# The down projection's seven block products: sums into the residual by accumulating transfers instead of by VectorE

## The chip, the cores and the metric

The kernel runs on one core of one Trainium2 chip. The metric is the device time of one execution in microseconds (us), as the median of several executions. In the profile the engines are called PE (TensorE's matmuls), PEld (TensorE's weight loads), DVE (VectorE), ACT (ScalarE), POOL (GpSimd) and SP (SyncE, which issues most transfers).

## The reference

A decoder trunk of two layers on 512 tokens of width 1024. Each layer has a mixer (a gated spatial mixer in layer 0, sliding-window attention in layer 1), a gated MLP with a causal depthwise convolution of width 3, and a gated per-layer embedding, each added to the residual `h`. The change touches the MLP's down projection alone:

```python
def conv_ffn(xn, w_up, conv_w, conv_b, w_down):
    h = xn @ w_up                                   # 1024 -> 2 x 2816
    hp = jnp.pad(h, ((0, 0), (CONV_WIDTH - 1, 0), (0, 0)))
    c = conv_b + sum(hp[:, t:t + S] * conv_w[t] for t in range(CONV_WIDTH))
    g, u = jnp.split(c, 2, axis=-1)
    return (jax.nn.silu(g) * u) @ w_down            # 2816 -> 1024
...
    h = h + conv_ffn(rmsnorm(h, norm_ffn[i]), ...)
```

## The kernel before

Everything is kept transposed: features on the 128 partitions, the 512 tokens along the row. The residual is eight tiles `h[0]` to `h[7]` of 128x512 float32 in SBUF. To reach float32 accuracy each operand is split into a high and a low part (`wh`, `wl` for weights: L197 the high part by a cast on ScalarE, L198 the rest by a subtraction on VectorE), and each product is three matmuls (L229).

Weights come as a planned list of pieces of up to 1 MB, loaded by SP's queue into three staging buffers (`wraw`, L167) and split into units of up to 1024 columns, four of which can be held at once (`WBUFS`). `pump` splits four units ahead of the one in use, so a split that is late by less than that lead stops nobody.

The 22 feature blocks of the MLP are handled in three parts of 8, 8 and 6 (`PARTS`). In a part, `up` makes two PSUM tiles per block, `gated` (L547 on) applies norm, convolution and gate, and then the part is projected down and added to the residual. The last part uses plain products (`dense_add`). The first two parts of each layer use `woven_add`: a matrix product of 2x2 blocks by seven block products instead of eight. There are four such stages in the program (two layers, two parts). A stage runs over four quarters `c`; a quarter makes two of the residual's tiles, `top` = `h[2c]` and `low` = `h[2c+1]`. Its weight sums (`wsum`, L157 to L159) are made by VectorE, too.

Each of the seven products is 12 matmuls of 128x128 on 256 columns. Two PSUM tiles take them: `chain` (in the profile `dx`, 256 columns) collects products 1, 6, 7 and 4 on top of each other, and ScalarE copies what stands in it between them: `head` after product 1 (first half, L509) and after 6 (second half, L514), `tail` after 7 (second half, L523) and after 4 (first half, L496). `other` (`dy`, 512 columns) holds product 2 in its first half and product 5 in its second, and product 3 goes on top of product 5. So product 3 cannot start before somebody has read the second half (L513 before), product 7 not before the second copy into `head`, and product 4 not before the first copy into `tail`. VectorE subtracts the second half of `other` from `low` (L513), adds `head` and `other` to `top` (L524, L525) and subtracts `tail` from `low` (L497). The fourth product of a quarter is put off into the next quarter (`late`), and the gate of the next part's first block stands after quarter 0 (`between`).

The tiles `head` (tag `acc`) and `tail` (tag `sq`) have two buffers each, so a quarter reuses those of two quarters before; the gate's tiles `c` use the tags `c0` and `c1`, two buffers each. The scheduler decides the order of each engine's instructions when the program is built; on the chip each engine goes through its list in that order and waits on semaphores.

Of the kernel before, what the change touches and what calls it, by code (L numbers as in the profile page):

```python
# [8 lines left out]
F32 = mybir.dt.float32  # L9
F32R = mybir.dt.float32r  # L10
AF = mybir.ActivationFunctionType
ALU = mybir.AluOpType

P = 128
D = 1024
S = 512
# [8 lines left out]
N = S // 2  # L25
# [25 lines left out]
def tile_yoco(ctx: ExitStack, tc: tile.TileContext, t, out: bass.AP, out_b: bass.AP):  # L51
    nc = tc.nc
# [7 lines left out]
    tp = ctx.enter_context(tc.tile_pool(name="tp", bufs=2))  # L60
# [4 lines left out]
    def psum(name):  # L65
        return mmp.tile([P, S], F32, tag="mm", name=name)
# [106 lines left out]
    def pump(upto):  # L173
        while state["unit"] < min(upto, len(units)):
            i, q, lo, n = units[state["unit"]]
            load(i + 1)
            u = state["unit"]
            own = pieces[i][3]
            if own:
                pool, *tags = own[q]  # L180
                wh, wl = (pool.tile([P, n], F32R, tag=tg, name=f"own{u}_{tg}") for tg in tags)
            else:
                wh = wp.tile([P, UNIT], F32R, tag="wh", bufs=WBUFS, name=f"wh{u}")
                wl = wp.tile([P, UNIT], F32R, tag="wl", bufs=WBUFS, name=f"wl{u}")
            if i in woven:
                src = weave(i, q)
                hi, low = (x[:, :n].rearrange("p (b k m) -> p b k m", b=src.shape[1], m=P) for x in (wh, wl))
            elif i in paired:
                whole = raws[i][:, : pieces[i][1]].rearrange("p (c k n) -> p k c n", c=2, n=256)
                src = whole[:, lo // S : (lo + n) // S]  # L190
                hi, low = (x[:, :n].rearrange("p (k c n) -> p k c n", c=2, n=256) for x in (wh, wl))
            else:
                src, hi, low = raws[i][:, lo : lo + n], wh[:, :n], wl[:, :n]
            if u == 0:
                cast = nc.vector.tensor_copy(hi, src)
            else:
                cast = nc.scalar.copy(hi, src)  # L197
            state["split"] = splits[u] = cast, nc.vector.tensor_sub(low, src, hi.bitcast(F32))  # L198
            ready[u] = (wh, wl, n)
            state["unit"] += 1  # L200

    def take():
        u = state["next"]
        pump(u + 1)
        state["next"] += 1
        return ready.pop(u)
# [11 lines left out]
    def mm3(ps, parts, xs, c0, n=P, first=True, last=True, lows_last=False, onto=False):  # L218


        todo = []
        for (wh, wl, off), (xh, xl) in zip(parts, xs):
            hi, low = (w[:, off + c0 : off + c0 + n] for w in (wh, wl))
            todo.append([(hi, xh), (hi, xl), (low, xh)])
        if lows_last:
            todo = [[t[j] for t in todo for j in (0, 2)], [t[1] for t in todo]]
        todo = [x for t in todo for x in t]
        for j, (w, x) in enumerate(todo):
            nc.tensor.matmul(ps, w, x, start=first and j == 0, stop=last and j == len(todo) - 1,  # L229
                             skip_group_check=onto)  # L230
# [19 lines left out]
    h = [hp.tile([P, S], F32, tag=f"h{k}", name=f"h{k}") for k in range(KD)]  # L250
# [25 lines left out]
    ps = psum("idle").rearrange("p (a b) -> p a b", a=4)  # L276
# [165 lines left out]
    first, second = slice(0, N), slice(N, S)  # L442
# [35 lines left out]
    def woven_add(pairs, between):  # L478


        ops = {x: [p.operand(x) for p in pairs] for x in range(1, 8)}
        n = len(pairs) * P

        def unit():
            pump(state["next"] + WBUFS)
            return take()

        def product(x, ps, w, at0, first=True):
            wh, wl = w[:2]
            mm3(ps, [(wh, wl, at0 + k * P) for k in range(len(pairs))], ops[x], 0, first=first,  # L490
                onto=not first)

        def close(c, chain, w, tail):
            def run():
                product(4, chain, w, 0, first=False)
                nc.scalar.copy(tail[:, first], chain)  # L496
                nc.vector.tensor_sub(h[2 * c + 1], h[2 * c + 1], tail)  # L497
            return run

        late = None  # L500
        for c in range(4):
            top, low = h[2 * c], h[2 * c + 1]
            chain, other = psum(f"dx{c}")[:, first], psum(f"dy{c}")
            head = tp.tile([P, S], F32, tag="acc", name=f"head{c}")
            tail = tp.tile([P, S], F32, tag="sq", name=f"tail{c}")
            w = unit()
            product(1, chain, w, 0)
            product(2, other[:, first], w, n)
            nc.scalar.copy(head[:, first], chain)  # L509
            w = unit()  # L510
            product(5, other[:, second], w, n)
            product(6, chain, w, 0, first=False)
            nc.vector.tensor_sub(low[:, second], low[:, second], other[:, second])  # L513
            nc.scalar.copy(head[:, second], chain)  # L514
            w = unit()
            if late:
                late()
            for x in (7, 3) if c == 3 else (3, 7):
                if x == 3:
                    product(3, other[:, second], w, n, first=False)  # L520
                else:
                    product(7, chain, w, 0, first=False)
                    nc.scalar.copy(tail[:, second], chain)  # L523
            nc.vector.tensor_add(top, top, head)  # L524
            nc.vector.tensor_add(top, top, other)  # L525
            late = close(c, chain, unit(), tail)
            if c == 0:
                between()
        late()

    def ffn(l, norm, nxt):
# [41 lines left out]
        for i, (j0, j1) in enumerate(PARTS):  # L573
            if i < WOVEN:
                edge = at.tile([P, PAIRS, 2, N], F32R, tag="vtl", name=f"edge{i}")
                pairs = []
                for p in range((j1 - j0) // 2):
                    pair = Pair(p, edge, f"act{i}_{p}")
                    pair.begin(up(j0 + 2 * p) if p else ahead)
                    pair.end(up(j0 + 2 * p + 1))  # L580
                    pairs.append(pair)
                pss, res = up(j1, later=True), []
                u = state["next"]
                woven_add(pairs, lambda: res.append(gated(j1, pss, (u + WBUFS + 1, u + WBUFS + 2))))
                ahead, = res
                continue
            act = [whole(SLOTS - 1, j0, ahead)]
            act += [whole(j - j0 - 1, j, up(j)) for j in range(j0 + 1, j1)]
            pe = ple_in_rows() if l else ple_in(l)
            dense_add(act, j1 - j0, nxt)  # L590
# [72 lines left out]
    for q, k0, k1 in FIRST:  # L663
# [12 lines left out]
        if (q, k1) == (0, KD):  # L676
# [7 lines left out]
            cast, low = state["split"]  # L684
# [62 lines left out]
    for c in range(4):  # L747
# [4 lines left out]
        for j in range(2):  # L752
            m = 2 * c + j
            ps = ups[j]
# [23 lines left out]
    ps = psum("turned")  # L778
    for i, (name, l) in enumerate((("ple_b_gate", 1), ("norm_final", 0))):
        c0 = VEC[name] + l * KD  # L780
# [286 lines left out]
    side = at.tile([P, 4 * S], F32, tag="vtl", name="side")  # L1067
# [290 lines left out]
```

## Time and profile before

| | |
|---|---|
| median of 3 runs | 1123.33 us (1122.11 to 1124.11) |
| the profiled execution | 1120.52 us, of which the span from first to last instruction is 1118.8 us |
| granted TensorE clock in it | 0.998 |
| PE busy | 1108.8 us, 99% of the span |
| DVE busy | 868.3 us, 78% |
| ACT busy | 568.9 us, 51% |
| POOL busy | 103.9 us, 9% |
| the four stages of seven products | from 241.9, 370.0, 798.4 and 926.8 us, some 41 us each |

How to read it: the rows of a timeline give start and duration in us, engine, line, operation, and the tiles as out<-in; a bracket tells how long the engine stood idle before the instruction and what ended that. A group row gives busy time, the mean in ns of one instruction, and the idle time before the group's instructions. Matmuls overlap: what one costs is seen from the distance between two starts, not from its duration. Therefore "busy 99%" does not say how much of the time TensorE was waiting a little between starts.

### The profile page before, as it was taken

How to read it: one execution, taken by the hardware profiler on the slowest of the kernel's cores; microseconds unless marked ns; L12 is line 12 of the kernel's file. 1: busy time of each engine (PE TensorE's matmuls, PEld its weight loads, DVE VectorE, ACT ScalarE, POOL GpSimd, SP SyncE). 2: the span in 40 equal slices, each digit the busy share in tenths (PEclk: the TensorE clock that was granted, in tenths of full speed). 3: DMA queues.
4: the chain of work that ended last, by engine and by line, in shares of the span. 5: the costliest groups of instructions: out<-in, count | busy, mean ns of one | idle time of the engine just before them, and what ended most of it. 6: DMA issues, size and time to landing. Idle time of an engine off the chain costs nothing.

```text
span 1118.8 us, 14875 instructions
## 1 busy us (share of the span) xinstructions
PE 1108.8 (99%) x5691; PEld 947.1 (85%) x5691; DVE 868.3 (78%) x1374; ACT 568.9 (51%) x936; POOL 103.9 (9%) x167
## 2 busy tenths in 40 slices
PE   9999999999999999999999999999999999999997
PEld 7888888889888998888888887888898889988876
DVE  5566449999788877657988997499997898785696
ACT  5733325545444544554656776255454445445543
POOL 1100210000000000022204451100000000000210
PEclk9999999999999999999999999999999999999999
DMA  8632313223331252333134224321244212522433
GB/s 296 135 114 76 113 48 113 76 76 123 142 113 39 76 189 69 101 113 113 63 88 132 76 57 151 111 93 71 76 151 136 90 38 76 189 85 88 148 103 86
DMA packets 35624, 118.40 MB, mean 106 GB/s; under 512 B 11800, under 2 KB 17440, under 8 KB 25056
## 3 DMA queue, kind: packets, MB, share of 16 engines
q1 hardware_dynamic: 34800, 116.19, 31.8%
q0 software_dynamic: 336, 0.79, 0.4%
q8 instruction: 45, 0.74, 0.3%
q10 hardware_dynamic: 416, 0.46, 0.1%
q14 instruction: 27, 0.22, 0.1%
HBM read 109.02 MB, written 2.11 MB: 99 GB/s over the span
## 4 chain that ended last, share of the span: by engine, by line
PE 68%; DVE 20%; ACT 4%; DMA 4%; issue 3%; POOL 0%; POOLq 0%; SPq 0%; ACTq 0%; DVEq 0%
PE up L229 26%; PE d L229 7%; PE dx L229 5%; DVE wl L198 5%; PE dy L229 4%; PE gate L229 4%; PE u L229 4%; PE q L229 3%; DVE c L558 3%; DVE c L559 2%; PE o L229 2%; DVE hs L551 2%; ACT wh L197 1%; PE v L241 1%; PE v L239 1%
## 5 line engine op out<-in xcount | busy, mean ns | idle before, releaser
L198 DVE TENSOR_TENSOR wl<-wraw,wh 128x1024 fp32r<-128x1024 f32 (+2 forms) x198 | 232.8, 1177 | 83.4 <-ACT wh L197 82.1
L197 ACT CAST wh<-wraw 128x1024 fp32r<-128x1024 f32 (+2 forms) x197 | 194.1, 990 | 147.9 <-PE up L229 56.1
L229 PE MATMUL up<-nf00h,wh 128*128 128x512 f32 x352 | 137.1, 390 | 0.0
L229 PE MATMUL up<-nf10h,wh 128*128 128x512 f32 x352 | 137.0, 389 | 0.0
L229 PE MATMUL up<-nf10l,wh 128*128 128x512 f32 x352 | 137.0, 389 | 0.0
L229 PE MATMUL up<-nf00l,wh 128*128 128x512 f32 x352 | 137.0, 389 | 0.0
L229 PE MATMUL up<-nf00h,wl 128*128 128x512 f32 x352 | 136.9, 389 | 0.0
L229 PE MATMUL up<-nf10h,wl 128*128 128x512 f32 x352 | 136.9, 389 | 0.0
L557 ACT ACTIVATE c<-hs,vec 128x512 f32<-128x512 f32 x88 | 71.6, 815 | 64.4 <-DVE hs L551 62.6
L558 DVE SCALAR_TENSOR_TENSOR c<-hs,vec,c 128x511 f32<-128x511 f32 x88 | 65.5, 747 | 20.4 <-ACT c L557 20.4
L229 PEld LDWEIGHTS up<-nf10h,wh 128*128 128x128 f32 x352 | 66.1, 188 | 13.7
L229 PEld LDWEIGHTS up<-nf00h,wl 128*128 128x128 f32 x352 | 66.1, 188 | 13.7
L229 PEld LDWEIGHTS up<-nf10l,wh 128*128 128x128 f32 x352 | 66.1, 188 | 13.7
L229 PEld LDWEIGHTS up<-nf00l,wh 128*128 128x128 f32 x352 | 66.1, 188 | 13.6
L229 PEld LDWEIGHTS up<-nf00h,wh 128*128 128x128 f32 x352 | 66.1, 188 | 13.6
L229 PEld LDWEIGHTS up<-nf10h,wl 128*128 128x128 f32 x352 | 66.1, 188 | 13.5
L559 DVE SCALAR_TENSOR_TENSOR c<-hs,vec,c 128x510 f32<-128x510 f32 x88 | 65.6, 748 | 2.2
L197 ACT CAST wh<-wsum 128x1024 fp32r<-128x1024 f32 x32 | 33.7, 1052 | 35.3 <-PE dy L229 11.3
L551 DVE TENSOR_TENSOR hs<-up,nf1rstd 128x512 f32<-128x512 f32 x44 | 30.1, 686 | 21.1 <-DMA nf1rstd<-nf1line 10.5
L551 DVE TENSOR_TENSOR hs<-up,nf0rstd 128x512 f32<-128x512 f32 x44 | 30.1, 686 | 20.9 <-DMA nf0rstd<-nf0line 10.4
L198 DVE TENSOR_TENSOR wl<-wsum,wh 128x1024 fp32r<-128x1024 f32 x32 | 39.1, 1221 | 9.3 <-ACT wh L197 9.2
L562 ACT ACTIVATE a<-c 128x512 f32<-128x512 f32 x44 | 27.7, 630 | 15.9 <-DVE c L559 15.8
(519 smaller groups left out, 2661.4 us busy)
## 6 DMA issues: line engine op xcount, KB each, us to landing
wraw<-in_w_up SPq DMA_DIRECT2D x44, 1024.0 KB, 4.8
wraw<-in_w_down SPq DMA_DIRECT2D x16, 1024.0 KB, 4.8
wraw<-in_w_gate SPq DMA_DIRECT2D x8, 1024.0 KB, 5.3
wraw<-in_w_down SPq DMA_DIRECT2D x8, 768.0 KB, 4.1
wraw<-in_w_u SPq DMA_DIRECT2D x4, 1024.0 KB, 10.8
wraw<-in_w_out SPq DMA_DIRECT2D x4, 1024.0 KB, 4.7
wraw<-in_w_q SPq DMA_DIRECT2D x4, 1024.0 KB, 4.8
wraw<-in_w_o SPq DMA_DIRECT2D x4, 1024.0 KB, 4.9
```

The costliest lines, as they stand in the source:

```text
L197: cast = nc.scalar.copy(hi, src)
L198: state["split"] = splits[u] = cast, nc.vector.tensor_sub(low, src, hi.bitcast(F32))
L229: nc.tensor.matmul(ps, w, x, start=first and j == 0, stop=last and j == len(todo) - 1, skip_group_check=onto)
L239: nc.tensor.matmul(ps, xh[:, s], wh[:, a:b], start=st, stop=False)
L241: nc.tensor.matmul(ps, xh[:, s], wl[:, a:b], start=False, stop=en)
L551: ins = nc.vector.tensor_mul(hs, ps, rstds[1])
L557: nc.scalar.activation(c, hs, AF.Identity, bias=v("conv_b", l * 2 * NJ + col), scale=cw[2])
L558: nc.vector.scalar_tensor_tensor(c[:, 1:], hs[:, : S - 1], cw[1], c[:, 1:], op0=ALU.mult, op1=ALU.add)
L559: nc.vector.scalar_tensor_tensor(c[:, 2:], hs[:, : S - 2], cw[0], c[:, 2:], op0=ALU.mult, op1=ALU.add)
L562: nc.scalar.activation(a, cs[0], AF.Silu)
```

## The change

All four updates of the residual leave VectorE. `onto` issues a transfer from SBUF to SBUF on GpSimd's queue that adds its source to its target. What is to be added must stand in SBUF, so ScalarE copies the two PSUM reads that VectorE made: `side` (128x256, negative, tag `c1`) and `rest` (128x512, tag `c0`). What is to be subtracted is copied with a factor of -1 (`minus`).

```diff
+        def onto(x, y):
+            nc.gpsimd.dma_start(x, y, accum_op=ALU.add)
+
+        def minus(x, ps):
+            nc.scalar.activation(x, ps, AF.Copy, scale=-1.0)
+
         def close(c, chain, w, tail):
             def run():
                 product(4, chain, w, 0, first=False)
-                nc.scalar.copy(tail[:, first], chain)
-                nc.vector.tensor_sub(h[2 * c + 1], h[2 * c + 1], tail)
+                minus(tail[:, first], chain)
+                onto(h[2 * c + 1], tail)
             return run
...
+            side = tp.tile([P, N], F32, tag="c1", name=f"side{c}")
+            rest = tp.tile([P, S], F32, tag="c0", name=f"rest{c}")
             w = unit()
             product(1, chain, w, 0)
             product(2, other[:, first], w, n)
...
             product(5, other[:, second], w, n)
             product(6, chain, w, 0, first=False)
-            nc.vector.tensor_sub(low[:, second], low[:, second], other[:, second])
+            minus(side, other[:, second])
+            onto(low[:, second], side)
             nc.scalar.copy(head[:, second], chain)
+            onto(top, head)
             w = unit()
...
                 else:
                     product(7, chain, w, 0, first=False)
-                    nc.scalar.copy(tail[:, second], chain)
-            nc.vector.tensor_add(top, top, head)
-            nc.vector.tensor_add(top, top, other)
+                    minus(tail[:, second], chain)
+            nc.scalar.copy(rest, other)
+            onto(top, rest)
             late = close(c, chain, unit(), tail)
```

The program as built has 64 instructions fewer on VectorE, 32 more on ScalarE and 64 transfers more on GpSimd's queue; SP's list is the same. TensorE's list has the same matmuls, and their order differs inside the four stages only.

## The prediction

> **What bounds the kernel now.** I read the page first, then the four stages that the change touches (by windows), then what TensorE waits for, then single starts in the timeline.
>
> ```profile
> PE 1108.8 (99%) x5691; PEld 947.1 (85%) x5691; DVE 868.3 (78%) x1374; ACT 568.9 (51%) x936; POOL 103.9 (9%) x167
> PE 68%; DVE 20%; ACT 4%; DMA 4%; issue 3%; POOL 0%; POOLq 0%; SPq 0%; ACTq 0%; DVEq 0%
> ...
> 241.90:283.00 41.10, 40.96 (x338) 40.41 (x337) 37.07 (x49) 21.05 (x36) 0.00 (x0) 1.00 0.39 132
> 798.40:839.90 41.50, 40.98 (x339) 40.43 (x338) 37.14 (x50) 20.94 (x35) 0.00 (x0) 1.00 0.39 131
> ...
> its engine sat idle before it (us, times) until:
>   DVE h L513: 1.4, 3
>   ACT tail L523: 1.1, 4
> ```
>
> The window rows give, after the stretch and its length, the busy time of PE, PEld, DVE, ACT and POOL, the granted clock, the DMA engines' share and GB/s. In a stage VectorE is at 37.1 of 41 us, the fullest engine beside TensorE, ScalarE is half empty and GpSimd does nothing. But VectorE's load is only worth what TensorE waits for it. The last rows are from the list of L229, the matmuls' line: the two causes of idle time in the whole program that belong to our stages add up to 2.5 us. With the small pauses that this list leaves out, some 3 to 4 us are there to be won, 0.3% of the time, whatever VectorE is spared.
>
> The starts show what one such wait costs:
>
> ```profile
> 242.07 0.40 PE L229 MATMUL dx<-edge,wh 128*128 128x256 f32 x2
> ...
> 247.67 0.28 PE L229 MATMUL dx<-act,wl 128*128 128x256 f32 x1
> 248.02 0.38 PE L229 MATMUL dy<-act_0h,wh 128*128 128x256 f32 x1
> 248.24 0.28 PE L229 MATMUL dy<-act_0l,wh 128*128 128x256 f32 x1
> 248.36 0.28 PE L229 MATMUL dy<-act_0h,wl 128*128 128x256 f32 x1
> ...
> 258.05 0.28 PE L229 MATMUL dx<-act,wl 128*128 128x256 f32 x1
> 258.18 0.38 PE L229 MATMUL dx<-act_1h,wh 128*128 128x256 f32 x1
> 258.40 0.28 PE L229 MATMUL dx<-act_1l,wh 128*128 128x256 f32 x1
> ...
> 260.06 0.28 PE L229 MATMUL dy<-act_0l,wh 128*128 128x256 f32 x1
> 260.41 0.38 PE L229 MATMUL dx<-act_2h,wh 128*128 128x256 f32 x1
> 260.63 0.28 PE L229 MATMUL dx<-act_2l,wh 128*128 128x256 f32 x1
> ...
> 283.09 0.40 PE L229 MATMUL up<-nf00h,wh 128*128 128x512 f32 x1
> ...
> 804.06 0.28 PE L229 MATMUL dx<-act,wl 128*128 128x256 f32 x1
> 804.79 0.39 PE L229 MATMUL dy<-act_0h,wh 128*128 128x256 f32 x1 [0.45 <-DVE h L513]
> 805.01 0.28 PE L229 MATMUL dy<-act_0l,wh 128*128 128x256 f32 x1
> ```
>
> Undisturbed starts lie 0.12 us apart (248.24, 248.36), so a product of 12 takes 1.44 us and the 28 products of a stage 40.3; this stage takes 283.09 - 242.07 = 41.0. Each pause costs the wait and about 0.10 more, since the first start behind it is 0.22 from the next.
>
> **The change, part by part.** VectorE loses four instructions a quarter:
>
> ```profile
> L524 DVE TENSOR_TENSOR h<-h,head 128x512 f32<-128x512 f32 x16 | 10.9, 683 | 0.0
> L497 DVE TENSOR_TENSOR h<-h,tail 128x512 f32<-128x512 f32 x16 | 10.9, 682 | 0.0
> L525 DVE TENSOR_TENSOR h<-h,dy 128x512 f32<-128x512 f32 x16 | 10.9, 679 | 0.2
> L513 DVE TENSOR_TENSOR h<-h,dy 128x256 f32<-128x256 f32 x16 | 6.6, 414 | 0.3
> L514 ACT COPY head<-dx 128x256 f32<-128x256 f32 x16 | 5.8, 366 | 0.0
> L604 ACT COPY pe<-pin 128x512 f32<-128x512 f32 x8 | 4.7, 582 | 2.7 <-PE pin L229 2.7
> L197 ACT CAST wh<-wsum 128x1024 fp32r<-128x1024 f32 x32 | 33.7, 1052 | 35.3 <-PE dy L229 11.3 <-PE dx L229 8.8 <-issue 7.6
> ```
>
> That is 39.3 us of VectorE's time in all, 9.8 a stage, of which TensorE sees only the following:
>
> - *Product 3 waits for L513* (VectorE reads the second half of `other` behind a weight split). At 248.02 this cost 248.24 - 247.67 - 0.24 = 0.33, at 804.79 it cost 0.71; the other two stages hardly wait. Now ScalarE's `side` reads it, and stands ahead of the next weight cast in ScalarE's list; product 5, the stage's third, is over at 242.07 + 3 x 1.44 + 0.2 = 246.6 (0.2 because a matmul ends later than the next begins), `side` (0.37 by L514's row) at 247.0, and product 3 is due at 247.67 + 0.12 = 247.8. Gain 1.04. But product 7 behind it then comes earlier and meets `head`, which ScalarE ends at 249.23 and 805.63:
>
> ```profile
> 248.87 0.36 ACT L514 COPY head<-dx 128x256 f32<-128x256 f32 x1
> ...
> 805.26 0.37 ACT L514 COPY head<-dx 128x256 f32<-128x256 f32 x1
> ```
>
>   Product 3 would end at 249.2 and 805.6, so a pause of about 0.07 and 0.10 appears in both places: 0.35 given back.
> - *Product 4 waits for `tail`* (L523), in each of four stages: 260.63 - 260.06 - 0.24 = 0.33, 1.32 together. Nothing in the instruction changed, but the scheduler's order did: product 4 of quarter 1 now stands behind product 6 of quarter 2, two products later. Gain 1.32.
> - *Product 7 waits for `head`* at 258.18: 258.40 - 258.05 - 0.24 = 0.11, four times. In the new order product 3 stands between. Gain 0.45.
>
> Sum: 1.04 - 0.35 + 1.32 + 0.45 = 2.46 us.
>
> What is added: ScalarE gets `side` (0.37) and `rest` (0.58 by the row of L604, a copy of that size from PSUM), 0.95 a quarter or 3.8 a stage, on 21 of 41 us. Its list is in order, so what matters is what stands behind them: the weight casts, 1.05 each. I went through quarter 1 by the built order: `side` waits for the stage's ninth product, over at 242.07 + 9 x 1.44 + 0.2 = 255.2, and the cast behind it for the tenth (256.5), which reads its buffer; `rest` waits for the twelfth (259.6), the cast behind it for the thirteenth (260.8). So both copies fall into waits and cost nothing; uncovered they would cost up to 15 us (16 x 0.95). I take 0.2 off for two more small pauses: 2.3.
>
> The transfers are the unknown: no accumulating one is in the trace. The nearest rows (KB, us from issue to landing), and GpSimd's own time to issue one:
>
> ```profile
> hT<-turned_a SPq DMA_DIRECT2D x16, 64.0 KB, 2.0
> q<-qhi SPq DMA_DIRECT2D x12, 128.0 KB, 2.3
> nf0rstd<-nf0line POOLq DMA_DIRECT2D x1, 256.0 KB, 3.7
> n0rstd<-n0line POOLq DMA_DIRECT2D x1, 256.0 KB, 6.1
> n0line<-n0rt POOLq DMA_DIRECT2D x1, 2.0 KB, 8.8
> ...
> 161.28 0.59 POOL L401 DMA_DIRECT2D nf0rstd<-nf0line  x1 [8.15 <-DMA nf0line<-nf0rt]
> 476.80 0.32 POOL L974 COPY prs<-nsink 128x4 f32<-128x4 f32 x2 [314.94 <-PE pin L229]
> ```
>
> From SBUF to SBUF 64 KB more cost 0.3, so 256 KB would take 2.9 on SP's queue and reading the target as well 1.2 more: 4.1. GpSimd's queue adds about 1 (3.7 to 6.1 for 256 KB): I take L = 5 us to landing, with 2.9 and 8.8 as ends. GpSimd's queue in layer 0 is empty from 161 to 476, so nobody stands behind these issues except the transfers themselves.
>
> Who waits for a landing? Buffers: `head`, `tail`, `side`, `rest`, and the gate's `c` behind them. Nearest is `rest` of quarter 1, which in the program as built must wait until `rest` of quarter 0 has landed. That one in turn is issued only when `head` of quarter 0 has landed, as both add to `top`. So two landings lie in a row: `head` done 249.3, issued 249.6 (I allow 0.3 for each handing over), landed 249.6 + L, `rest` issued 0.3 later, landed 249.9 + 2L. With L = 5 that is 259.9, and `rest` of quarter 1 is wanted at 259.6: met almost exactly. How late may it be? Behind it in ScalarE's list stand the cast (1.05) and `tail`'s copy (0.37), which product 4, now the 18th of the stage and due at 242.07 + 17 x 1.44 = 266.6, waits for. 266.6 - 0.06 - 0.37 - 1.05 - 0.58 = 264.5. So landings are hidden up to 249.9 + 2L = 264.5, **L = 7.3 us**; beyond, each us more costs 2 us a stage, 8 in all. All other buffers come round after two quarters or with one landing, and have more room. On VectorE the first tile of the next part waits for `head` and `tail` of quarters 2 and 1, with the last split of the stage behind it; a landing at 5 ends that wait before the split's own buffer is free.
>
> The DMA engines: 16 transfers a stage add 3.7 MB to the 5.4 MB (132 GB/s x 41 us) that take a share of 0.39 now, so 0.26 more, or 0.53 if the target's bytes count again: 0.65 to 0.92, under 1.
>
> One rule speaks against the change. The Trainium skill, SBUF — State Buffer, section "SBUF: two separate sides", says that a transfer issued by GpSimd starves while VectorE runs an instruction in a two-port mode, because GpSimd cannot write the descriptors, and gives about 620 ns alone against 3100 ns beside such a copy. By it L would be 7.5 in an estimate, just past the limit, and 1.6 us lost in place of nothing. The same page, section "Who interferes with whom", has tensor_tensor without such a mode, and the VectorE rows quoted above are TENSOR_TENSOR; no run here shows an accumulating transfer beside them. By that rule the first rival would be the case.
>
> **The rivals.**
>
> 1. *Landings take too long* (slower): L above 7.3. GpSimd must write each transfer out while VectorE works, and the 16 DMA engines are shared with the weight loads. For it: the slowest of GpSimd's transfers took 8.8, and the share worked out above may reach 0.9. Against: 3.7 at the same size, and 2.3 for half of it on SP's queue. At 8.8 the loss is 8 x 1.5 = 12.0, less 2.3: +9.7, 1133.0. Chance 0.25.
> 2. *GpSimd cannot keep pace* (slower): four issues in a quarter of 41.0 / 4 = 10.25 us; if an accumulating issue holds it over 2.6 us, its queue sets the stage. At 3 us: 16 x 3 - 41 = 7 a stage, +28, 1151. Against: 0.59 for the issue above. Chance 0.06.
> 3. *Pauses only move* (no gain): ScalarE, through which all PSUM reads now go, meets TensorE elsewhere; the gain is 0 to 1: 1122.3 to 1123.3. For it: `head` already gives back 0.35. Chance 0.12.
>
> That the change doesn't do what it says can be left out: the built program has 64 fewer instructions on VectorE and 64 transfers more.
>
> **How the numbers follow.** The forecast, chance 0.57, is a gain of 2.3 us: 1118.2 in the profiled execution in place of 1120.52, and 1121.0 on the median of 1123.33 (that execution lies 2.8 under the median, within what runs differ by). Its own range is a gain of 1 to 3.7, 1122.3 to 1119.6, the upper end if the small pauses go as well. About 0.2%, 2.25 us, is what a measurement of this kernel can tell from no change; the forecast lies on that bound, so its 0.57 splits: 0.33 faster by more, 0.24 within. With rival 3 "same" has 0.36; rivals 1 and 2 make 0.31 slower. The range reaches from 1119.6 to rival 1 at its end, 1133.0, and leaves out rival 2 and a landing over 8.8, some 0.15.
>
> **What would show it.** Right: no VectorE rows on `dy`; the stages at 40.4 to 40.6 us from first to last product; VectorE at 27 us and ScalarE at 25 us in each; landings on GpSimd's queue near 5 us; no ScalarE wait on `rest`'s landing of over 4 us. Wrong: landings above 7.3 with ScalarE idle before `rest` of quarter 1 and a hole in TensorE's starts at product 4; or GpSimd busy for most of a stage, its transfers going out later quarter by quarter.

## The result and the profile after

The changed kernel takes **1119.35 us** (median of 7 runs, 1118.44 to 1120.37); the kernel before, run beside it, 1122.11 us (7 runs, 1120.20 to 1124.11). The ratio is **0.9974, 95% interval 0.9964 to 0.9984**: a gain of 2.9 us, 1.8 to 4.0. A second measurement (e10_after_again, below) gave 0.9966 [0.9954, 0.9979]. The forecast was 1121.0, 2.3 us below the median then known, 1123.33; the measured time lies 0.25 us below the low end of the range, 1119.6.

The profiled execution of the changed kernel took 1119.52 us. Busy times by engine and the first line of the chain of work that ended last, from its page:

```profile
PE 1108.5 (99%) x5691; PEld 947.7 (85%) x5691; DVE 835.3 (75%) x1310; ACT 584.8 (52%) x968; POOL 161.5 (14%) x231
...
PE 93%; DVE 3%; ACT 1%; issue 1%; DMA 1%; POOLq 0%; POOL 0%; ACTq 0%; DVEq 0%; SPq 0%
```

VectorE falls from 20% to 3% of the chain. That share is a weak sign: the kernel before has 11% in its second profile (e1_null), and e5_butside, which gains nothing, has 6%. The first of the four stages by windows (columns as in the prediction: stretch, length, PE, PEld, DVE, ACT, POOL, granted clock, DMA share, GB/s):

```profile
242.30:283.30 41.00, 41.00 (x339) 40.64 (x338) 29.52 (x34) 24.78 (x43) 12.12 (x14) 1.00 0.79 192
```

VectorE has 7.5 us less than before (37.07), ScalarE 3.7 more (21.05), GpSimd 12.1 in place of nothing, and the DMA engines' share doubled from 0.39. The starts in the first stage:

```profile
242.44 0.40 PE L229 MATMUL dx<-edge,wh 128*128 128x256 f32 x2
...
248.04 0.28 PE L229 MATMUL dx<-act,wl 128*128 128x256 f32 x1
248.16 0.28 PE L229 MATMUL dy<-act_0h,wh 128*128 128x256 f32 x1
...
258.36 0.28 PE L229 MATMUL dy<-act_0h,wh 128*128 128x256 f32 x1
...
261.24 0.40 PE L229 MATMUL dx<-edge,wh 128*128 128x256 f32 x2
261.61 0.39 PE L229 MATMUL dx<-edge,wl 128*128 128x256 f32 x1
261.83 0.39 PE L229 MATMUL dx<-edge,wh 128*128 128x256 f32 x2
...
283.11 0.40 PE L229 MATMUL up<-nf00h,wh 128*128 128x512 f32 x1
```

Product 3 follows at 248.16 without a pause. ScalarE had read its buffer by 246.92 + 0.39 = 247.31:

```profile
246.92 0.39 ACT L497 ACTIVATE side<-dy 128x256 f32<-128x256 f32 x1 [0.47 <-PE dy L229]
```

Product 3 of quarter 1 (258.36) follows without a pause too, and now stands where product 7 waited for `head` at 258.18 before. The stage is 283.11 - 242.44 = 40.67 us long. The other three, read from their first and last starts in the same way, are 40.66 or 40.67 too; before they were 41.02, 40.86, 41.41 and 40.85. One pause is new: at 261.61 and 261.83 two starts follow late, 0.37 (for two matmuls, 0.24 undisturbed) and 0.22 instead of 0.12. VectorE's rows show what they wait for, the low part of the weights that quarter 2 starts with, ended at 260.32 + 1.23 = 261.55:

```profile
258.52 0.69 DVE L158 TENSOR_TENSOR wsum<-wsum,wraw 128x512 f32<-128x512 f32 x1
259.12 0.69 DVE L573 TENSOR_TENSOR a<-a,c 128x512 f32<-128x512 f32 x1
259.72 0.69 DVE L159 TENSOR_TENSOR wsum<-wsum,wraw 128x512 f32<-128x512 f32 x1
260.32 1.23 DVE L198 TENSOR_TENSOR wl<-wraw,wh 128x1024 fp32r<-128x1024 f32 x1
```

The accumulating transfers by landing (KB each, median us from issue to landing), in the page's list of issues:

```profile
h<-head POOLq DMA_DIRECT2D x16, 256.0 KB, 4.2
h<-rest POOLq DMA_DIRECT2D x16, 256.0 KB, 6.7
h<-tail POOLq DMA_DIRECT2D x16, 256.0 KB, 6.7
...
h<-side POOLq DMA_DIRECT2D x16, 128.0 KB, 4.7
```

Single landings lie between 2.7 and 9.9 us, with a median of 4.9 over all 64. GpSimd's time to issue them, with what GpSimd waited for, in its timeline of the first stage:

```profile
249.91 0.87 POOL L494 DMA_DIRECT2D h<-head  x1 [1.35 <-ACT head L523]
253.70 0.85 POOL L494 DMA_DIRECT2D h<-rest  x1 [2.93 <-ACT head L517]
...
264.04 0.85 POOL L494 DMA_DIRECT2D h<-rest  x1 [3.69 <-DMA h<-head]
266.63 0.86 POOL L494 DMA_DIRECT2D h<-side  x1 [1.74 <-ACT side L497]
268.89 0.86 POOL L494 DMA_DIRECT2D h<-head  x1 [1.40 <-ACT head L523]
270.34 0.86 POOL L494 DMA_DIRECT2D h<-tail  x1 [0.59 <-ACT tail L497]
```

A bracket names what came last by the profile. For `rest` that is not always what counts: `head` of quarter 0 landed at 253.17, and in all 16 quarters `rest` goes out 0.52 to 0.56 us after the landing of its quarter's `head`, whatever the bracket says.

### The profile page after: what moved, and what is told of

Same layout as the page of the kernel before. It is cut to its first block, busy times and chain, and to the rows that moved or that the text cites. A ratio compares the mean times of both kernels' runs of the same rounds, so it can differ in the third digit from the quotient of the medians.

```text
span 1117.8 us, 15039 instructions
## 1 busy us (share of the span) xinstructions
PE 1108.5 (99%) x5691; PEld 947.7 (85%) x5691; DVE 835.3 (75%) x1310; ACT 584.8 (52%) x968; POOL 161.5 (14%) x231
## 4 chain that ended last, share of the span: by engine, by line
PE 93%; DVE 3%; ACT 1%; issue 1%; DMA 1%; POOLq 0%; POOL 0%; ACTq 0%; DVEq 0%; SPq 0%
PE up L229 43%; PE d L229 9%; PE dx L229 8%; PE dy L229 6%; PE gate L229 4%; PE u L229 4%; PE o L229 4%; PE v L239 1%; PE v L241 1%; PE v L240 1%; PE q L229 1%; PE pin L229 1%; PE k L229 1%; PE gt L239 1%; PE gt L241 1%
## 5 line engine op out<-in xcount | busy, mean ns | idle before, releaser
L198 DVE TENSOR_TENSOR wl<-wraw,wh 128x1024 fp32r<-128x1024 f32 (+2 forms) x198 | 232.6, 1178 | 103.0 <-ACT wh L197 102.5
L229 PE MATMUL up<-nf00h,wh 128*128 128x512 f32 x352 | 137.1, 390 | 0.0
L229 PE MATMUL up<-nf10h,wh 128*128 128x512 f32 x352 | 137.0, 389 | 0.0
L229 PE MATMUL up<-nf10l,wh 128*128 128x512 f32 x352 | 137.0, 389 | 0.0
L229 PE MATMUL up<-nf00l,wh 128*128 128x512 f32 x352 | 137.0, 389 | 0.0
L229 PE MATMUL up<-nf00h,wl 128*128 128x512 f32 x352 | 136.9, 389 | 0.0
L229 PE MATMUL up<-nf10h,wl 128*128 128x512 f32 x352 | 136.9, 389 | 0.0
L229 PEld LDWEIGHTS up<-nf00h,wh 128*128 128x128 f32 x352 | 66.1, 188 | 13.7
L229 PEld LDWEIGHTS up<-nf10h,wl 128*128 128x128 f32 x352 | 66.1, 188 | 13.7
L229 PEld LDWEIGHTS up<-nf10h,wh 128*128 128x128 f32 x352 | 66.1, 188 | 13.7
L229 PEld LDWEIGHTS up<-nf00l,wh 128*128 128x128 f32 x352 | 66.1, 188 | 13.6
L229 PEld LDWEIGHTS up<-nf10l,wh 128*128 128x128 f32 x352 | 66.1, 188 | 13.6
L229 PEld LDWEIGHTS up<-nf00h,wl 128*128 128x128 f32 x352 | 66.1, 188 | 13.6
L494 POOL DMA_DIRECT2D h<-side x16 | 13.9, 870 | 372.7 <-ACT side L497 372.7
L198 DVE TENSOR_TENSOR wl<-wsum,wh 128x1024 fp32r<-128x1024 f32 x32 | 38.9, 1224 | 22.7 <-ACT wh L197 22.5
L561 DVE TENSOR_TENSOR hs<-up,nf0rstd 128x512 f32<-128x512 f32 x44 | 30.1, 687 | 19.5 <-DMA nf0rstd<-nf0line 10.4
```

The lines of the kernel that those rows point to most:

```text
L494: nc.gpsimd.dma_start(x, y, accum_op=ALU.add)
L561: ins = nc.vector.tensor_mul(hs, ps, rstds[1])
```

## The experiments

**Theory 1**, after the result: what counts is the one PSUM read that product 3 waits for (the second half of `other`). Once ScalarE makes it, product 3 is ready early, and the scheduler's order of products has room for the others. The accumulating transfers neither win nor cost anything by themselves. **Rival A**: what counts is how much work VectorE has lost. **Rival B**: the order of the products alone does it. Ratios are to the kernel before on the same chip, and the stages' lengths are from each kernel's profiled execution.

### e1_null: the kernel before, again

Only a comment is changed.

> The kernel before with nothing changed but a comment, to see its scatter and a second profile. Theory 1 (the change removes TensorE's pauses in the four stages, 1.5 us between the two profiles at hand, and the timed difference of 2.9 us is larger because these pauses are longer in other executions): ratio 1.000 within 0.1%, and at least one of the four stages is longer here than in the first profile (41.0, 40.9, 41.4, 40.9 us), by 0.3 us or more. Rival (the rest of the timed difference lies outside the stages or is scatter): ratio 1.000 within 0.1%, the stages again 40.8 to 41.4.

Measured: 1122.49 us (11 runs) against 1122.44 (19 runs), ratio 0.9997 [0.9989, 1.0006]; stages 41.59, 40.85, 41.83, 40.85. Two stages are longer than in the first profile by 0.3 us or more, as Theory 1 expected. What ended TensorE's idle time in the whole program, from the list of L229 of this run, and the starts at product 3:

```profile
  DVE h L513: 3.4, 4
  ACT tail L523: 1.1, 4
```

```profile
248.01 0.28 PE L229 MATMUL dx<-act,wl 128*128 128x256 f32 x1
248.92 0.39 PE L229 MATMUL dy<-act_0h,wh 128*128 128x256 f32 x1 [0.63 <-DVE h L513]
249.14 0.28 PE L229 MATMUL dy<-act_0l,wh 128*128 128x256 f32 x1
```

The wait for `tail` is the same as in the first profile (1.1), the one for L513 is 3.4 in place of 1.4. (The list counts rows of PE and of PEld each.) At this product the pause costs 249.14 - 248.01 - 0.24 = 0.89 where the first profile had 0.33; in the third stage, worked out likewise, 1.13 instead of 0.71. So the pauses at product 3 are not a constant: how late L513 is depends on how far VectorE's list happens to stand behind TensorE's. It starts 5.5 us after the stage's first matmul in the first profile (242.07) and 6.0 us after it here (242.41):

```profile
247.55 0.41 DVE L513 TENSOR_TENSOR h<-h,dy 128x256 f32<-128x256 f32 x1
```

```profile
248.45 0.41 DVE L513 TENSOR_TENSOR h<-h,dy 128x256 f32<-128x256 f32 x1
```

The first profile, of an execution of 1120.52 us, was one with short pauses.

### e4_order: the order alone

Each product's first matmul is ordered behind the last of the product before it in the written order, which is the order that the changed kernel has as built. Nothing else changes: VectorE still makes the four updates.

```diff
+        line = []
...
-            mm3(ps, [(wh, wl, at0 + k * P) for k in range(len(pairs))], ops[x], 0, first=first,
-                onto=not first)
+            done = mm3(ps, [(wh, wl, at0 + k * P) for k in range(len(pairs))], ops[x], 0, first=first,
+                       onto=not first)
+            if line:
+                behind(done[0], line[-1])
+            line.append(done[-1])
```

> The kernel before, its products held to the order that the changed kernel has; VectorE keeps all reads and sums. Theory 1: tail's pause goes (1.3 us) but product 3 waits for VectorE's read in quarter 1 as well, where VectorE is latest, some 1 to 3 us a stage: stages 41 to 43 us, ratio 1.000 to 1.008. Rival B (order alone): stages 40.6 to 40.8, ratio 0.997 to 0.9985. Rival A: no change, 1.000.

Measured: 1142.92 us (4 runs), ratio 1.0178 [1.0165, 1.0192]; stages 45.84, 45.58, 47.45 and 46.43. Rival B falls: the order alone costs 20 us. Theory 1 had the wait in the right place, but its size was missed by far (a ratio of 1.000 to 1.008 expected): the wait is over 3 us in every stage in place of 1 to 3, and many starts behind it are slow (last section). TensorE and VectorE in the first stage of this kernel:

```profile
258.35 0.28 PE L228 MATMUL dx<-act,wl 128*128 128x256 f32 x1
262.05 0.48 PE L228 MATMUL dy<-act_0h,wh 128*128 128x256 f32 x1 [3.41 <-DVE h L516]
```

```profile
258.63 0.69 DVE L158 TENSOR_TENSOR wsum<-wsum,wraw 128x512 f32<-128x512 f32 x1
259.23 0.69 DVE L566 TENSOR_TENSOR a<-a,c 128x512 f32<-128x512 f32 x1
259.83 0.69 DVE L159 TENSOR_TENSOR wsum<-wsum,wraw 128x512 f32<-128x512 f32 x1
260.44 1.22 DVE L198 TENSOR_TENSOR wl<-wraw,wh 128x1024 fp32r<-128x1024 f32 x1
261.57 0.42 DVE L516 TENSOR_TENSOR h<-h,dy 128x256 f32<-128x256 f32 x1
```

Product 3 of quarter 1 is ready to go at 258.47; its buffer's read (L516 here, L513 before) stands behind an unbroken row of the gate's and the weights' instructions and ends at 261.99. The kernel before put product 7, product 4 and parts of quarter 2 into this hole; I take its order for the scheduler's answer to that read, though no trace shows a scheduler's reasons. In the changed kernel `side` reads the same buffer at 256.18 on ScalarE, and the short order is free to be used.

### e5_butside: everything but that read

The changed kernel, with the second half of `other` read and subtracted by VectorE as before.

```diff
-            minus(side, other[:, second])
-            onto(low[:, second], side)
+            nc.vector.tensor_sub(low[:, second], low[:, second], other[:, second])
```

> The changed kernel with `side` left as it was: head, tail and rest go by ScalarE and accumulating transfers (12 of the 16 in a stage), the second half of `other` is read and subtracted by VectorE (L513 of before). VectorE then has some 8 us a stage less than before, but the read that product 3 waits for is still in its list, behind a weight split. Theory 1 (what counts is which engine reads that buffer, and the order of products that follows from it): the pauses at products 3, 4 and 7 stay, stages of 40.8 to 41.3 us, ratio to before 0.9985 to 1.0005. Rival A (what counts is how much work VectorE has lost): most of the gain stays, stages of 40.6 to 40.7, ratio 0.997 to 0.998.

Measured: 1122.17 us (11 runs), ratio 0.9993 [0.9984, 1.0002]; stages 41.11, 40.86, 41.60 and 40.87, as in the kernel before. The list of idle causes of L229 has both old rows again:

```profile
  DVE h L520: 1.8, 3
  ACT tail L497: 1.1, 4
```

VectorE's busy time in the stages is 30.7 us on average there (36.3 before, over the same stretches), and the time did not move. Rival A falls. TensorE's order of matmuls in the four stages is, one by one, that of the kernel before again: with this one read back on VectorE, the old order comes back.

### e2_side and e9_side_vec: that read alone

Both start from the kernel before. In e2_side the read goes by ScalarE into `side`, and an accumulating transfer adds it; `head`, `tail` and the second read stay VectorE's. In e9_side_vec VectorE adds `side` from SBUF instead, with no transfer.

```diff
+            side = tp.tile([P, N], F32, tag="c1", name=f"side{c}")
...
-            nc.vector.tensor_sub(low[:, second], low[:, second], other[:, second])
+            minus(side, other[:, second])
+            onto(low[:, second], side)
```

> Of the change only side: ScalarE reads the second half of other and an accumulating transfer subtracts it; head, other and tail stay VectorE's. Theory 1 (what counts is that the PSUM read for which product 3 waits leaves VectorE's list): the pause at product 3 is gone and with it the scheduler's reordering, so tail's pause goes too; stages 40.6 to 40.9 us, ratio 0.997 to 0.9985. Rival A (VectorE's load counts: 9.8 us less a stage): only 1.7 us of the 9.8 are taken off, so a sixth of the gain, ratio 0.9993 to 1.000. Rival B (the order of the products alone counts): the same order but for one split, so all of the gain.

> The smallest cut: ScalarE copies the second half of `other` into `side` (16 copies of 128x256 in all), VectorE adds `side` from SBUF, and everything else, `tail`, `head` and the second half of the sum into `top` included, is as in the kernel before; no accumulating transfer. Theory 1 (the one PSUM read that product 3 waits for, and the order of products that follows): the whole gain, stages 40.5 to 40.6 as in e2_side and e3_reads, ratio to before 0.9965 to 0.9980. Rival (e2_side's gain came from the transfer taking 6.6 us from VectorE): pauses at product 3 or at the split weights come back, stages 40.8 to 41.2, ratio 0.9985 to 1.0000.

Measured: e2_side 1119.78 us (7 runs), ratio 0.9976 [0.9965, 0.9987], stages 40.53 to 40.55; e9_side_vec 1119.95 us (10 runs), ratio 0.9975 [0.9965, 0.9984], stages 40.54 or 40.55. Sixteen copies of 128x256, some 0.37 us each, bring the whole gain, together with the order that the scheduler makes of them: TensorE's order in both is that of the changed kernel but for one matmul. The read without the new order was not run. As I read the starts, the pauses at products 4 and 7 (1.32 and 0.45 us) went with the order and those at product 3 with the read; that split is argued, not shown. The VectorE of e9_side_vec does as much in the stages as before, in the same stretch in both kernels (before first, then e9_side_vec):

```profile
242.00:282.50 40.50, 40.36 (x334) 39.80 (x333) 36.97 (x49) 20.76 (x34) 0.00 (x0) 1.00 0.39 133
```

```profile
242.00:282.50 40.50, 40.50 (x336) 40.18 (x335) 37.57 (x50) 23.30 (x40) 0.00 (x0) 1.00 0.38 132
```

VectorE does even 0.6 us more, and TensorE is busy in all of the stretch.

### e3_reads: all reads by ScalarE, all sums by VectorE

The changed kernel with `onto` turned into an addition on VectorE.

```diff
         def onto(x, y):
-            nc.gpsimd.dma_start(x, y, accum_op=ALU.add)
+            nc.vector.tensor_add(x, x, y)
```

> ScalarE makes side and rest as in the change, but VectorE adds all four from SBUF; no accumulating transfer. VectorE keeps as many and as long instructions as before. Theory 1 (only the PSUM reads matter, who adds does not): stages 40.6 to 40.9 us, ratio 0.997 to 0.9985. Rival A (VectorE's load counts): no gain, stages 41.0 or more, ratio 0.9995 to 1.001. Rival B (order alone): nearly the order of the changed kernel, so all of the gain.

Measured: 1119.58 us (7 runs), ratio 0.9971 [0.9961, 0.9982]; stages 40.55 or 40.56. Without the 64 transfers the stages are 0.12 shorter than the changed kernel's, one late start less, and the total is the same within what can be measured. e2_side, with 16 of the transfers, has stages as short. The transfers are not where the gain is from.

### e10_after_again: the changed kernel, again

> The changed kernel itself again, beside the runs of before on this chip, to fix the size of the change: if the first measure (a gain of 2.8 us) was a fluke of its runs, the ratio is 0.9980 to 0.9990 (the gain of 2.3 us forecast, or less); if the first profile of before showed too short pauses at product 3, as e1_null says (stages of 165.1 in place of 164.1), it is 0.9965 to 0.9978, and the stages are 40.67 again.

Measured: 1119.21 us (5 runs) against 1122.65 (14 runs), ratio 0.9966 [0.9954, 0.9979]; stages 40.66 to 40.68. The gain was no fluke: 3.4 us between these medians.

### e6_chain3: one landing more in a row

The changed kernel with one transfer of zeros more a quarter, added to the first columns of `top` between `head` and `rest`.

```diff
+        zeros = const.tile([P, P], F32, tag="zeros", bufs=1, name="zeros")
+        nc.gpsimd.memset(zeros, 0.0)
...
             onto(top, head)
+            onto(top[:, :P], zeros)
```

> The changed kernel with one more accumulating transfer in each quarter (128x128 zeros, 64 KB, onto the first columns of `top`) between `head` and `rest`, so that three landings lie in a row ahead of `rest` of the quarter after the next buffer. In the changed kernel `rest` of quarter 0 landed at about 260.8, and the limit worked out in the prediction is 264.5. Theory 1 with that limit: the added landing takes 3 to 5 us, `rest` of quarter 0 lands at 264 to 266, ScalarE waits for it about 4 us longer, and product 4 of quarter 1 pauses by 0 to 1.5 us; the same in the next quarters: 0 to 10 us in all, ratio to before 0.997 to 1.006, with the pause at the place named and ScalarE's wait for the landing of `rest` over 4 us. Rival (a landing never reaches TensorE, the limit is wrong): no pause there, ScalarE catches up, ratio 0.997 to 0.998. Were landings independent of each other, `rest` would still land near 261.

Measured: 1139.56 us (4 runs), ratio 1.0149 [1.0136, 1.0163]; stages 43.11, 46.29, 43.80, 46.65. A landing does reach TensorE, but not at the place that I had named, and it costs 20 us against the changed kernel where I had expected 10 at most. GpSimd's timeline in the first stage:

```profile
259.50 0.85 POOL L494 DMA_DIRECT2D h<-rest  x1 [5.30 <-DMA h<-zeros]
260.05 1.19 POOL L494 DMA_DIRECT2D h<-side  x1
260.59 1.52 POOL L494 DMA_DIRECT2D h<-head  x1
261.29 1.71 POOL L494 DMA_DIRECT2D h<-tail  x1
...
271.87 0.86 POOL L494 DMA_DIRECT2D h<-rest  x1 [5.49 <-DMA h<-zeros]
...
273.51 1.88 POOL L494 DMA_DIRECT2D h<-tail  x1
...
285.32 0.86 POOL L494 DMA_DIRECT2D h<-rest  x1 [2.04 <-DMA h<-zeros]
```

`rest` is issued every 12.4 and 13.5 us (271.87 - 259.50, 285.32 - 271.87), while TensorE needs a quarter in 10.2. Each wait for a landing holds GpSimd's whole list, so `side`, `head` and `tail` of the next quarter pile up behind it, go out together (0.54 to 0.70 us apart), and land late. In the changed kernel a quarter of GpSimd's list had 1.74 + 1.40 + 0.59 = 3.7 us in which it waited only for ScalarE (its timeline above): that was its spare, and one more landing, 2.0 to 5.5 us of waiting and 0.86 of issue, uses it up. What GpSimd waited for in the whole run (us, times, the longest), from the list of waits:

```profile
POOL h L494 <- DMA h<-head: 76.1, 16, 8.5
POOL h L494 <- DMA h<-zeros: 60.2, 14, 5.7
```

In the changed kernel the list names such a wait only once (3.7 us), but by the landings each `rest` waits for `head` there as well (above). So the changed kernel waits for one landing in each quarter, and this build for two in a row.

TensorE feels it at the end of the stage, at the last product, which waits for a copy of `tail` that waits for its buffer (ScalarE, then TensorE):

```profile
283.50 0.38 ACT L497 ACTIVATE tail<-dx 128x256 f32<-128x256 f32 x1 [3.50 <-DMA h<-tail]
```

```profile
283.94 0.39 PE L229 MATMUL dx<-act_2h,wh 128*128 128x256 f32 x1 [2.20 <-ACT tail L497]
```

### e7_vec_two_pauses and e8_dma_two_pauses: the pauses that are left

e7 is e3_reads (sums on VectorE), e8 the changed kernel (sums by transfers), both with two edits: the third sum of a unit's weights is made when it is needed for the first time and not with the first two, and the next weight cast stands behind `head`'s second copy in ScalarE's list. So the third sum is made later, where the expectation of e7 calls it earlier.

```diff
+        if q == 2:
+            s = sums[i]
             nc.vector.tensor_add(s[:, 1], s[:, 2], g[:, 2])
...
-            nc.scalar.copy(head[:, second], chain)
+            copied = nc.scalar.copy(head[:, second], chain)
...
             w = unit()
+            behind(state["split"][0], copied)
```

> e3_reads (all four reads by ScalarE, all four additions by VectorE, no accumulating transfer) with two waits more removed: the third weight sum of a unit (VectorE) is made one step earlier, and the next weight cast stands behind the copy of `head` in ScalarE's list, which product 7 waits for. Theory 1: the pauses at products 7 (0.18 + 0.10) and at the unit behind the fourth product go or shrink, stages 40.55 to 40.2-40.4, that is 0.6 to 1.4 us less than e3_reads, ratio to before 0.9960 to 0.9968. Rival (pauses only move): stages stay at 40.5, ratio 0.997.

> The changed kernel (accumulating transfers) with the same two waits removed as in e7. Theory 1 (a landing is hidden, the transfers neither win nor cost anything by themselves): stages 40.2 to 40.4, ratio 0.9960 to 0.9970, the same as e7 within 0.7 us. Rival (the DMA share of 0.8 delays weight loads or VectorE's operands): at least 0.1 us a stage slower than e7, 0.5 us or more in all.

Measured: e7 1118.00 us (5 runs), ratio 0.9957 [0.9944, 0.9971], stages 40.35; e8 1118.43 us (5 runs), ratio 0.9956 [0.9944, 0.9969], stages 40.31. The floor of 337 starts (28 products of 12, and the next matmul) is 336 x 0.12 = 40.3; one start in each stage of e8 and two of e7 are still late. The stages of both are shorter than the changed kernel's (40.66) and e3_reads' (40.55). In total both are faster than the kernel before; against the changed kernel (0.9974 and 0.9966) the intervals overlap, so a further gain in total is not shown. Nor were the two edits run apart. e7 and e8 agree although their first stages look like this (e7, then e8):

```profile
242.00:282.50 40.50, 40.50 (x336) 40.24 (x335) 37.17 (x51) 25.46 (x44) 0.00 (x0) 1.00 0.34 120
```

```profile
242.00:282.50 40.50, 40.50 (x339) 40.41 (x338) 29.51 (x34) 24.76 (x43) 12.12 (x14) 1.00 0.79 197
```

With VectorE at 37.2 of 40.5 us the stage is within 0.1 us of its floor, and with VectorE at 29.5 it is there as well. What VectorE does in a stage is covered in both, and a DMA share of 0.79 costs the stages nothing that can be seen.

## Why the prediction was right, and where it was wrong

The mechanism and the places of the gain came as forecast, and the change is a small gain. The measured time lies below the range because of two steps: the price of the wait at product 3 (1.04 us, read from one execution; 2.02 in the next profile of the same kernel), and the base of 1123.33 from which the gain was subtracted (1122.1 to 1122.65 with more runs). A third term, 0.2 off for small pauses, was too small by 0.7 and hid part of the first. Step by step:

- **Product 3 no longer waits for L513**: right, 248.16 follows 248.04. The *size* was the step that failed. I took 1.04 us from one profiled execution, of 1120.52 us, which is below all three runs then known (1122.11 to 1124.11), and subtracted the sum from a median 2.8 us above it. The next profile of the same kernel (e1_null, 1122.49, close to the median) has 0.89 + 1.13 = 2.02 at these two places, twice as much. That is one more profile; what the term is in most executions stays open.
- **Product 7 meets `head`, 0.35 given back**: right. In the changed kernel the start there lies 0.18 behind the one before it and the next 0.22 behind that, so 0.16 is lost in each stage, 2 x 0.16 = 0.32 in the two places named. The second and fourth stages had lost 0.14 and 0.12 there before, so 0.38 is new in all.
- **Product 4 and `tail`, 1.32; product 7 after `head` of quarter 1, 0.45**: right, both pauses are gone in all four stages. e4_order corrects the reason: the new order is no gain by itself. It is only usable since the read of product 3's buffer is early; with that read on VectorE the same order costs 3.7 us a stage at this one product.
- **0.2 off for two small pauses**: too little. The new pause at the weights that quarter 2 starts with is 261.83 - 261.24 - 3 x 0.12 = 0.23 a stage, 0.9 together. I had followed ScalarE's list by the built order and not VectorE's: three weight sums and two gate instructions stand ahead of that split, and the new order asks for its result earlier (19.0 us after the stage's first start in place of 19.5). In e7 and e8, where the third sum is made later, the pause is gone.
- The stages add up to 162.67 us in the changed kernel, 164.14 in the first profile of before and 165.12 in e1_null: 1.5 or 2.5 us less, depending on which execution one subtracts from. With the sizes above the steps give the same: 1.04 - 0.38 + 1.32 + 0.45 - 0.9 = 1.5, and 2.5 with 2.02 in place of 1.04. So it is luck that the forecast of 2.3 lies near the larger one: two terms were off by 1.0 and 0.7 in opposite directions. The measured gains, by the ratios 2.9 (1.8 to 4.0) and 3.8 (2.4 to 5.2), both hold 2.5 in their intervals, and neither holds 1.5. What is left, 0.4 to 1.4, no profile shows: outside the four stages the two profiled executions of the kernel before took 954.7 and 955.5 us, those of the changed kernel (first profile and e10_after_again) 955.1 and 954.8. These stretches scatter by as much: the attention between the stages took 387.45 us in the first profile of before and 388.45 in e1_null. Whether the change does anything there stays open.
- **The base**: 1123.33 was the median of three runs; with 7 to 19 runs the kernel before is at 1122.1 to 1122.65. The gain, 2.8 and 3.4 us between the medians of the two measurements, lay inside the forecast's own 1 to 3.7, but the range's low end was set with the largest gain from a base that was itself about 1 us high. From the 1122.11 measured beside the change the same forecast would have been 1119.8, within 1118.4 to 1121.1, and 1119.35 lies in there. The uncertainty of the base had no place in it.
- **ScalarE's two copies fall into waits**: right; 24.8 us a stage (25 forecast), and e3_reads, with the same copies, has no new pause on them.
- **Stages at 40.4 to 40.6 us**: 40.66 and 40.67; the new pause of 0.23 makes the difference. No row of VectorE on `dy` is left, as forecast.
- **VectorE at 27 us a stage**: 28.4 to 29.5. The four rows' durations add up to 39.3, but VectorE's total fell by 868.3 - 835.3 = 33.0 only, and the durations of its other rows add up to the same in both profiles within 0.8. In a row without gaps the end of one instruction lies over the start of the next by about 0.1 us (rows above: 258.52 + 0.69 = 259.21, the next start is 259.12), so an instruction taken out of it saves less than its duration.
- **Landings, L = 5**: right in the middle (median 4.9 over all 64), too short for `rest` and `tail` (medians 6.7). `head` was issued at 249.91, `rest` of quarter 0 at 253.70, and ScalarE waited for its landing until 260.93:

```profile
260.93 0.59 ACT L534 COPY rest<-dy 128x512 f32<-128x512 f32 x1 [0.64 <-DMA h<-rest]
```

  249.9 + 2L = 260.9 gives L = 5.5 on average, `head` 3.8 and `rest` up to 7.2; forecast 259.9, limit 264.5. The wait of 0.64 was hidden by what stands before product 4, as worked out. Later landings of up to 9.9 were hidden too. But the limit was read from one buffer. e6_chain3 shows that the list of the engine that waits for the landings can run out first, as each wait holds everything behind it; in that build `rest` of quarter 1 (260.10) did not wait at all.
- **The DMA share of 0.65 to 0.92**: 0.79. **GpSimd's issue**: 0.85 to 0.94 us each where its queue was free, above the 0.59 of the nearest row, four a quarter 3.4 of 10.2; rival 2 was right to be small, though its true form is the one of e6_chain3.
- **The rule that spoke against the change** did not show. GpSimd's issues are as long beside VectorE's work as without it: 0.87 at 249.91 and 0.86 at 268.89 lie beside a split (L198, a TENSOR_TENSOR), 0.85 at 253.70 beside a SCALAR_TENSOR_TENSOR, and 0.85 at 264.04 falls where VectorE is idle. No run has these transfers without VectorE's work, so a small delay of the landings is not excluded. The Trainium skill, SBUF — State Buffer, ties the starving to VectorE's two-port modes (section "SBUF: two separate sides") and has no such mode for tensor_tensor (section "Who interferes with whom"); the issues beside the splits agree with that.
- **Rival 3, pauses only move**, was part of the truth: of the 2.8 us that went (3.8 with e1_null's pauses), 0.4 came back at product 7 and 0.9 at the weights that quarter 2 starts with.

One reading was careless: the 2.5 us of the two causes of idle time came from a list that counts rows of PE and PEld each. For PE alone it has 0.4 at L513. The sum was made from starts and does not rest on it, and what there was to win, 164.14 - 161.24 = 2.9 us by the first profile and 165.12 - 161.24 = 3.9 by e1_null, with e8's stages for the floor, was "3 to 4" all the same.

## What to carry to other kernels

Before an engine is relieved of work, look for the one instruction of its that the bounding engine waits for, and at what stands ahead of it in its list; here 16 copies of 0.37 us brought all that 64 moved instructions brought. A pause that depends on how far one list stands behind another differs from execution to execution, so it is priced from several profiles, and a gain is subtracted from the kind of execution that it was read in. Where an in-order list waits for landings, its spare time per round has to be counted as well as the buffer that is next to be used: in e6_chain3 it ran out first.

## What the runs showed of the hardware

- After a pause of 3.7 us TensorE falls to about half speed. In e4_order 15 to 26 starts behind each of the four pauses are 0.213 apart in place of 0.12 (in the second stage from the fifth start on), and the granted clock of that stretch in the first stage is 0.57 (stretches as above):

```profile
258.00:262.00 4.00, 0.63 (x6) 0.43 (x4) 4.00 (x8) 1.85 (x4) 0.00 (x0) 1.00 0.01 4
262.00:266.00 4.00, 3.95 (x20) 3.96 (x21) 3.02 (x4) 0.00 (x0) 0.00 (x0) 0.57 0.01 4
```

  So about 7 of the 20 us that e4_order lost (some 80 starts by 0.093) are not waiting but the slow starts behind it. In e6_chain3 a pause of 2.48 us left the spacing at 0.12, behind one of 2.97 the last two starts of the stage were slow, and behind those of 4.46 and 4.95 all starts to the end of the stage were. The Trainium skill, TensorE: Matmul & The Clock Gate, section "What's actually happening", puts the change to half clock at an idle window of about 3.4 us that runs free of the kernel. The length agrees: the granted clock is 0.50 from 262.19 to 265.60 in e4_order. But the pause of 2.97 us was enough without an idle window of that length: there the clock is 0.50 from 849.48 to 852.89, and TensorE had been busy for 1.27 of the 3.41 us before.
- Accumulating transfers within SBUF (256 KB) landed after 4.2 to 6.7 us by the medians, and took 0.85 to 0.94 us of GpSimd each when its queue was free. In a bunch the recorded issues are longer, 1.19, 1.52, 1.71 and up to 1.88 in e6_chain3's timeline, but they overlap: one starts 0.54 to 0.70 us after the other. The 16 transfers of a stage raised the DMA engines' share by 0.40 of 41 us, and the largest group of weight loads (`in_w_up`) landed after 5.7 instead of 4.8 us by the median (5.0 in e8, with as many transfers), for which TensorE did not wait.
